# Steps of a gated recurrence, and two sums of weights, each placed behind one split of v's weights

## The chip, the cores and the metric

The kernel runs on one core of a Trainium2 chip. The core has a matrix engine (PE, with PEld loading its weights), a vector engine (DVE), a scalar engine (ACT), a general engine (POOL) and a queue engine (SP); SP and POOL issue the DMAs. Each engine takes its own instructions in order and waits on semaphores for the others. The metric is the time of one execution in microseconds on the device; the median of several executions is compared.

## The reference

One layer of a hybrid block for 512 tokens of width 1024. The normalised input is projected to the inputs of three mixers and their gates; the three results are projected, gated, added, projected again, and a SwiGLU feed-forward layer follows. Two mixers matter here.

```python
xc = causal_conv(u_lru)                          # width 4, per channel
r, i = sigmoid(gate_r(xc)), sigmoid(gate_i(xc))
log_a = -8 * r * softplus(-lam)
a, mult = exp(log_a), sqrt(-expm1(2 * log_a))
h[t] = a[t] * h[t - 1] + mult[t] * i[t] * xc[t]  # the recurrence, along 512 tokens

q, k, v = normalised_x @ w_q, @ w_k, @ w_v       # 1024 x 1024 each, for the attention
```

## The kernel before

Every product in float32 precision is made from three passes of PE over rounded parts: a matrix is split into a high part (ACT rounds it, `whi`, L141) and a low part (DVE subtracts the high part from the raw matrix, `wlo`, L142), and PE adds high*high, high*low and low*high. `split_w` (L134) makes both parts of one piece of weights. The high and the low parts each have three buffers, so that the split of piece n+3 cannot start before PE has used piece n.

The projections to v, k and q (in this order, `VKQ`) go by a Strassen-like scheme with seven products (`ORDER`: 11, 12, S2, S1, S3, S4, 22) in place of eight. Each product has two pieces of weights of 128x1024 (i = 0, 1), and PE makes 12 matmuls of 512 columns for a piece. I write (S4,0) for piece 0 of product S4. `add_seven` (L202) lists the 14 pieces of a unit; the unit numbers un = 0, 1, 2 are v, k and q. Some pieces take more than a split: with product 11 DVE adds two raw blocks to a new block `qs` (L214), which is the raw block of S2; with product S4 DVE adds `qs` to the raw block of 12 (L209), and the sum is the raw block of S4. When the last raw use of a block is over, its buffer takes a block of the next unit (`seven_load`, SP's queue, and an adding DMA on POOL's).

`tok_product` (L820) issues the matmuls. Between products the result is put together from PSUM: `snap` (L841) copies a bank on ACT, `final` (L849) adds or subtracts another bank on DVE. In the traces these are the tile `r` at L843 and L851. Four PSUM tiles exist for this.

The recurrence runs in four chunks of 256 channels (c = 0 to 3), of which the first two are done before v. What remains of chunks 2 and 3 is done while PE works on v:

- `lru_exp`: exponentials and a square root on ACT (L690, L693).
- `lru_decay`: one DVE instruction (L698) and, for chunks 2 and 3, one ACT instruction `1 - t` (L702).
- `lru_input`: two DVE instructions, in these notes "root" (L706) and "product" (L707).
- `lru_scan`: two DVE scans of 512 tokens (L713).
- `lru_store`: a split of the result, ACT (L719) and DVE (L720), and two DMAs to memory on POOL's queue (L722).

The order of each engine's instructions is made by a planner before the run. It follows the program with its own estimate of durations and gives an engine, each time it is free, the ready instruction of the highest priority. Priority is the position in which the program text issues an instruction; `tc.high_priority(n)` moves it n positions up. Splits of v are moved up 320 positions, those of k and q 200, snaps 300, finals and steps of the recurrence not at all. `tc.issue_after(ins)` puts the instructions of its block behind `ins` in the order of that engine, without a wait for its end. Small steps wait in a list `bg`, and `tick` takes one of them at fixed places between the matmuls. `weights` (L297) emits the splits some two pieces ahead of their use.

Before, the list holds for the time of v: decay of chunk 2, decay of chunk 3, the two input steps of chunk 2 (L773), and, from the end of product S3 on, the input steps of chunk 3, scan of chunk 2, scan of chunk 3 behind the fifth last low part emitted until then (L881 to L886), and the two stores (L887).

Of the kernel before, what the change touches and what calls it, by code (L numbers as in the profile page):

```python
# [11 lines left out]
AF = mybir.ActivationFunctionType  # L12
ALU = mybir.AluOpType
# [51 lines left out]
def layer_kernel(ctx: ExitStack, tc: tile.TileContext, x, xt, vecs, w_in, w_qkv7, w_gate7, w_pool, w_rg, w_ig,  # L65
                 w_branch, w_br7, w_out, w_fg, w_fu, w_fd, w_fd7, out):
    nc = tc.nc
    act = nc.scalar.activation
    dve = nc.vector
# [59 lines left out]
        return [wp.tile([P, 1024], F32R, tag=tag, name=n)  # L129
                for tag, n in (("whi", nh), ("wlo", nl))]  # L130

    los = []

    def split_w(raw, shape, n):  # L134
        hi, lo = weight_tiles("whi" + n, "wlo" + n)
        if len(shape) == 3:
            hi, lo = (t.rearrange("p (a b) -> p a b", a=shape[1]) for t in (hi, lo))
        else:
            hi, lo = (t.rearrange("p (a b c) -> p a b c", a=shape[1], b=shape[2]) for t in (hi, lo))
        with tc.high_priority(60):  # L140
            act(hi, raw, AF.Copy)  # L141
            los.append(dve.tensor_tensor(lo, raw, hi.bitcast(F32), ALU.subtract).ins)  # L142
        return hi, lo

# [33 lines left out]
    VKQ = (2, 1, 0)  # L178
# [23 lines left out]
    def add_seven(un, nm, i):  # L202
        u, pieces, shape = UNITS[un]
        last = i == pieces - 1

        def make(n):
            if nm == "S4":
                r = qraw[u, "12", i]
                dve.tensor_tensor(r, r, qraw[u, "S2", i], ALU.add)  # L209
            src = qraw[u, {"S1": "21", "S3": "11", "S4": "12"}.get(nm, nm), i]  # L210
            parts = split_w(src, [P] + list(shape), n)
            if nm == "11":
                qraw[u, "S2", i] = r = b4(list(shape), f"qs{u}{i}")
                dve.tensor_tensor(r, qraw[u, "21", i], src, ALU.add)  # L214
                add = nc.gpsimd.dma_start(src, seven_src(u, "21", i), accum_op=ALU.add)
            if last:
                if un < 3:
                    seven_load(un + 1, {"S1": ("21",), "S3": ("11",), "S4": ("12",), "22": ("22",)}.get(nm, ()))
                elif un == 3 and nm == "11":
                    with tc.issue_after(add.ins):  # L220
                        seven_load(un + 1, ("21", "11"))
                elif un == 3:
                    seven_load(un + 1, {"12": ("12",), "S2": ("22",)}.get(nm, ()))
            return parts
        specs.append((("seven", u, nm, i), make))
# [211 lines left out]
    with ExitStack() as first:  # L437
# [258 lines left out]
        def lru_decay(c):  # L696
            e, t = lru[c]["r"], lru[c]["t"]
            dve.scalar_tensor_tensor(t, e, 1.0, t, ALU.add, ALU.mult)  # L698
            if c < 2:
                dve.tensor_scalar(t, t, -1.0, 1.0, ALU.mult, ALU.add)  # L700
            else:
                act(t, t, AF.Identity, scale=-1.0, bias=1.0)  # L702

        def lru_input(c):
            e, s_ = lru[c]["r"], lru[c]["s"]
            dve.scalar_tensor_tensor(s_, e, 1.0, s_, ALU.add, ALU.mult)  # L706
            dve.tensor_tensor(s_, s_, lru[c]["i"], ALU.mult)  # L707

        def lru_scan(c):
            t, s_ = lru[c]["t"], lru[c]["s"]  # L710
            h = lru[c]["i"]
            for j in range(2):
                dve.tensor_tensor_scan(h[:, j, :], t[:, j, :], s_[:, j, :], 0.0, ALU.mult, ALU.add)  # L713
            lru[c] = h

        def lru_store(c):
            y = lru.pop(c)
            h, l = b4([2, S], f"yh{c}", "b", F32R), y.bitcast(F32R)
            act(h, y, AF.Copy)  # L719
            dve.tensor_tensor(l, y, h.bitcast(F32), ALU.subtract)  # L720
# [49 lines left out]
        gate1(1)  # L770
        step(of(lru_scan, 1)), step(g3, of(lru_store, 0)), step(t3, of(lru_store, 1)), step(of(lru_exp, (2, 3)))
        gate1(2)
        for f, c in ((lru_decay, 2), (lru_decay, 3), (lru_input, 2)):  # L773
            step(of(f, c))
        bg.extend(prepare_t())
        gate1(3)

# [57 lines left out]
        for t in VKQ:  # L835
            ps = {}
            r = {}
# [21 lines left out]
            for nm in ORDER:  # L859
# [38 lines left out]
        for cc in range(2):  # L898
# [6 lines left out]
            lo, hi = slice(0, H), slice(H, S)  # L905
# [7 lines left out]
            for nm in ORDER:  # L913
                ps, half, first_, t, ts_, src, ss = plan[nm]
# [330 lines left out]
    with ExitStack() as third:  # L1245
# [9 lines left out]
        lo, hi = slice(0, H), slice(H, S)  # L1255
# [61 lines left out]
    with ExitStack() as ffn:  # L1317
# [18 lines left out]
        for c in range(4):  # L1336
# [10 lines left out]
            for j in range(2):  # L1347
# [3 lines left out]
                t = x1p[c // 2, j][:, c % 2, :]  # L1351
# [78 lines left out]
        raw = {}  # L1430
# [124 lines left out]
        for m in range(4):  # L1555
            t = fp.tile([P, 2, S], F32, tag="mm", name=f"ps_d{m}")
# [198 lines left out]
```

## Time and profile before

| | us |
|---|---|
| median of three executions | 867.79 (867.76 to 868.42) |
| the profiled execution | 867.76 |
| its span, first to last instruction | 866.0 |
| PE busy | 858.7 (99%) |
| DVE busy | 735.7 (85%) |
| ACT busy | 522.9 (60%) |
| v's matmuls, first to the first of k | 139.19 to 176.73 |

The profile is of one execution; all times in it are microseconds from the first instruction. A busy PE is modelled and is not by itself PE at its best pace, so the starts of successive matmuls are read. A row of the timeline gives the start, the duration, the engine, the line, the operation, the tiles (out<-in), the count, and in brackets the idle time in front of it with what ended it. In a row of the waits stand the total, the count and the longest.

### The profile page before, as it was taken

What the parts mean: (1) busy time and instruction counts of PE and PEld (TensorE: products, weight loads), DVE (VectorE), ACT (ScalarE), POOL (GpSimd) and SP (SyncE); (2) the same over time, 40 slices, a digit from 0 to 9 for tenths busy, and PEclk for the clock granted to TensorE, in tenths of its full rate; (3) what the DMA queues carried; (4) which work ended last, traced back from release to release, by engine and by line L of the source; (5) the groups of instructions that cost most, each with busy time, mean ns of one, the idle gap of its engine ahead of it and who ended that gap; (6) DMA issues with size and microseconds to landing.
All of it is one profiled execution on the core that took longest, in us unless ns stands there. A gap on an engine that the chain in (4) does not pass through costs nothing.

```text
span 866.0 us, 14235 instructions
## 1 busy us (share of the span) xinstructions
PE 858.7 (99%) x5563; PEld 789.7 (91%) x5563; DVE 735.7 (85%) x937; ACT 522.9 (60%) x727; POOL 90.8 (10%) x130
## 2 busy tenths in 40 slices
PE   9999999999999999999999999999999999999998
PEld 7888878888899988889889988889999999999998
DVE  7899897998796698877897787699988888899974
ACT  7554989557966567546665545464555555755642
POOL 1110002232433101000001100000000000121200
PEclk9999999999999999999999999999999999999999
DMA  9586356799592876644727855345633433797913
GB/s 343 164 288 204 98 164 184 228 313 259 172 305 77 245 217 222 216 126 154 218 87 177 195 168 178 100 140 141 166 102 98 121 100 120 225 244 202 196 38 122
DMA packets 116643, 154.08 MB, mean 178 GB/s; under 512 B 8160, under 2 KB 90080, under 8 KB 116576
## 3 DMA queue, kind: packets, MB, share of 16 engines
q1 hardware_dynamic: 103904, 107.30, 38.5%
q0 software_dynamic: 12528, 45.62, 22.2%
q8 instruction: 43, 0.70, 0.3%
q10 hardware_dynamic: 144, 0.26, 0.1%
q14 instruction: 24, 0.20, 0.1%
HBM read 132.71 MB, written 18.87 MB: 175 GB/s over the span
## 4 chain that ended last, share of the span: by engine, by line
PE 88%; DVE 5%; ACT 4%; issue 1%; DMA 1%; SPq 0%; DVEq 0%; ACTq 0%
PE ps_y L315 11%; PE ps_x L315 8%; PE ps_q L830 7%; PE ps_dy L1674 6%; PE ps_dx L1674 5%; PE ps_br L307 3%; PE ps_br L306 3%; PE ps_br L308 3%; PE ps_bY L1299 2%; PE ps_gy L315 2%; PE ps_gate L733 2%; DVE wlo L142 2%; PE ps_bX L1299 2%; PE ps_gx L315 2%; PE ps_pool L307 2%; PE ps_pool L306 2%
## 5 line engine op out<-in xcount | busy, mean ns | idle before, releaser
L141 ACT ACTIVATE whi<-raw 128x1024 fp32r<-128x1024 f32 x69 | 72.8, 1055 | 82.7 <-PE ps_br L307 17.4
L142 DVE TENSOR_TENSOR wlo<-raw,whi 128x1024 fp32r<-128x1024 f32 x69 | 84.2, 1221 | 26.2 <-ACT whi L141 25.5
L142 DVE TENSOR_TENSOR wlo<-qw,whi 128x1024 fp32r<-128x1024 f32 x48 | 58.3, 1220 | 15.8 <-ACT whi L141 15.8
L141 ACT ACTIVATE whi<-qw 128x1024 fp32r<-128x1024 f32 x48 | 50.3, 1053 | 28.2 <-PE ps_q L830 13.2
L1460 ACT ACTIVATE wh_S<-w_S 128x1024 fp32r<-128x1024 f32 x36 | 38.3, 1064 | 30.3 <-PE ps_y L315 18.3
L1580 POOL DMA_DIRECT2D dw<-in_w_down_dram x20 | 16.9, 862 | 305.4 <-DVE wl L1461 243.1
L1461 DVE TENSOR_TENSOR wl_S<-w_S,wh_S 128x1024 fp32r<-128x1024 f32 x36 | 43.8, 1220 | 3.3 <-ACT wh_S L1460 3.3
L1460 ACT ACTIVATE wh<-w 128x1024 fp32r<-128x1024 f32 x27 | 28.6, 1060 | 28.7 <-PE ps_x L315 9.1
L1461 DVE TENSOR_TENSOR wl<-w,wh 128x1024 fp32r<-128x1024 f32 x27 | 32.9, 1220 | 8.2 <-ACT wh L1460 8.2
L1460 ACT ACTIVATE whdS<-dw 128x1024 fp32r<-128x1024 f32 x20 | 21.2, 1061 | 20.6 <-PE ps_dy L1674 10.6
L1113 DVE TENSOR_TENSOR_SCAN E<-K,ahead 128x512 f32<-128x512 f32 (+3 forms) x32 | 25.4, 814 | 5.8 <-ACT K L1109 5.8
L1461 DVE TENSOR_TENSOR wldS<-dw,whdS 128x1024 fp32r<-128x1024 f32 x20 | 24.3, 1222 | 5.1 <-ACT whdS L1460 5.0
L306 PE MATMUL ps_lru<-HH,whi 128*128 128x512 f32 x64 | 24.6, 384 | 0.0
L306 PE MATMUL ps_br<-yph,whi 128*128 128x512 f32 x64 | 24.5, 383 | 0.0
L306 PE MATMUL ps_pool<-HH,whi 128*128 128x512 f32 x64 | 24.5, 383 | 0.0
L306 PE MATMUL ps_br<-yHH,whi 128*128 128x512 f32 x64 | 24.5, 383 | 0.0
L306 PE MATMUL ps_gate<-HH,whi 128*128 128x512 f32 x64 | 24.4, 381 | 0.0
L307 PE MATMUL ps_br<-yHL,whi 128*128 128x512 f32 x64 | 24.4, 381 | 0.0
L307 PE MATMUL ps_lru<-HL,whi 128*128 128x512 f32 x64 | 24.3, 379 | 0.0
L308 PE MATMUL ps_lru<-HH,wlo 128*128 128x512 f32 x64 | 24.3, 379 | 0.0
L307 PE MATMUL ps_gate<-HL,whi 128*128 128x512 f32 x64 | 24.3, 379 | 0.0
L308 PE MATMUL ps_gate<-HH,wlo 128*128 128x512 f32 x64 | 24.3, 379 | 0.0
(740 smaller groups left out, 3435.9 us busy)
## 6 DMA issues: line engine op xcount, KB each, us to landing
raw<-in_w_in_dram SPq DMA_DIRECT2D x31, 512.0 KB, 5.2
qw<-in_w_qkv_dram SPq DMA_DIRECT2D x24, 512.0 KB, 6.8
dw<-in_w_down_dram POOLq DMA_DIRECT2D x20, 512.0 KB, 8.2
w<-in_w_ffn_gate_dram SPq DMA_DIRECT2D x36, 256.0 KB, 3.5
w<-in_w_ffn_up_dram SPq DMA_DIRECT2D x36, 256.0 KB, 4.3
raw<-in_w_branch_dram SPq DMA_DIRECT2D x16, 512.0 KB, 4.0
qw<-in_w_qkv_dram POOLq DMA_DIRECT2D x12, 512.0 KB, 7.5
qd<-r POOLq DMA_DIRECT2D x12, 512.0 KB, 7.1
```

The costliest lines, as they stand in the source:

```text
L141: act(hi, raw, AF.Copy)
L142: los.append(dve.tensor_tensor(lo, raw, hi.bitcast(F32), ALU.subtract).ins)
L306: nc.tensor.matmul(ps, lh, rh, start=start, stop=False, skip_group_check=skip)
L307: nc.tensor.matmul(ps, lh, rl, start=False, stop=False, skip_group_check=skip)
L308: nc.tensor.matmul(ps, ll, rh, start=False, stop=stop, skip_group_check=skip)
L315: nc.tensor.matmul(o, a_[a][:, w, k, :], il2(b_[b][:, k, :]), start=first and n == k == 0, stop=last and n == 2 and k == 3, skip_group_che ...
L830: nc.tensor.matmul(ps[:, a, :], b_[:, k, ts_], il(a_[:, kk, :]), start=first and n == k == 0, stop=n == 2 and k == 3, skip_group_check=True)
L1113: dve.tensor_tensor_scan(E[:, c0:c0 + n][:, ::-1], K[:, c0 + 1:c0 + n + 1][:, ::-1], ahead[:, S - n:][:, ::-1], 0.0, ALU.mult, ALU.add)
L1299: nc.tensor.matmul(o, ah[x_][:, w, k, :], il2(b[k][y_]), start=first_ and n == k == 0, stop=n == 2 and k == 3, skip_group_check=True)
L1460: act(h, src, AF.Copy)
L1461: dve.tensor_tensor(l, src, h.bitcast(F32), ALU.subtract)
L1674: nc.tensor.matmul(o, a_[a][:, w, k0 + k, :], il2(b_[b][:, k, :]), start=first and i == k == 0, stop=last and i == 2 and k == nk - 1, skip ...
```

## The change

`marks` now keeps the high and the low instruction of each split of a unit, and `behind_split` names steps that are issued within the making of one of v's pieces, each behind its low part on DVE. They carry the priority of v's splits.

- behind (12,0): decay of chunk 3
- behind (12,1): root of chunk 2
- behind (S2,0): product of chunk 2
- behind (S2,1): the ACT ends of both decays (`1 - t`), behind the high part on ACT
- behind (S1,1): root of chunk 3
- behind (S4,0): product of chunk 3
- behind (S4,1): scan of chunk 2
- behind (22,0): scan of chunk 3

The two sums for S4 (L209) are put behind the low part of v's (S2,1); for k and q this says nothing. The decay of chunk 2 stays in the list. The two stores enter the list after k's product 11 and not after v's product S3. No arithmetic is changed.

```diff
-    los = []
+    his, los, marks, behind_split = [], [], {}, {}
...
-            act(hi, raw, AF.Copy)
+            his.append(act(hi, raw, AF.Copy).ins)
...
                 r = qraw[u, "12", i]
-                dve.tensor_tensor(r, r, qraw[u, "S2", i], ALU.add)
+                with tc.issue_after(marks[0, "S2", 1][1]):
+                    dve.tensor_tensor(r, r, qraw[u, "S2", i], ALU.add)
...
+            marks[un, nm, i] = his[-1], los[-1]
+            for f in behind_split.pop((un, nm, i), ()):
+                with tc.issue_after(los[-1]):
+                    f()
...
-            else:
+
+        def lru_decay_end(c):
+            t = lru[c]["t"]
+            with tc.issue_after(marks[0, "S2", 1][0]):
                 act(t, t, AF.Identity, scale=-1.0, bias=1.0)
...
-        def lru_input(c):
+        def lru_root(c):
             e, s_ = lru[c]["r"], lru[c]["s"]
             dve.scalar_tensor_tensor(s_, e, 1.0, s_, ALU.add, ALU.mult)
+
+        def lru_product(c):
+            s_ = lru[c]["s"]
             dve.tensor_tensor(s_, s_, lru[c]["i"], ALU.mult)
...
-        for f, c in ((lru_decay, 2), (lru_decay, 3), (lru_input, 2)):
-            step(of(f, c))
+        step(of(lru_decay, 2))
+        behind_split.update({(0, "12", 0): [of(lru_decay, 3)], (0, "12", 1): [of(lru_root, 2)],
+                             (0, "S2", 0): [of(lru_product, 2)],
+                             (0, "S2", 1): [of(lru_decay_end, 2), of(lru_decay_end, 3)], (0, "S1", 1): [of(lru_root, 3)],
+                             (0, "S4", 0): [of(lru_product, 3)], (0, "S4", 1): [of(lru_scan, 2)],
+                             (0, "22", 0): [of(lru_scan, 3)]})
...
-                if (t, nm) == (VKQ[0], "S3"):
-                    def last_scan():
-                        with tc.issue_after(los[-5]):
-                            lru_scan(3)
-
-                    step(of(lru_input, 3)), step(of(lru_scan, 2)), step(last_scan)
+                if (t, nm) == (VKQ[1], "11"):
                     step(of(lru_store, 2)), step(of(lru_store, 3))
```

More of the change, by code (lines that the diff above doesn't have):

```diff
@@ L700, in lru_decay, with lru_input, lru_scan @@
                 dve.tensor_scalar(t, t, -1.0, 1.0, ALU.mult, ALU.add)
-            else:
+        def lru_decay_end(c):
+            t = lru[c]["t"]
+            with tc.issue_after(marks[0, "S2", 1][0]):
                 act(t, t, AF.Identity, scale=-1.0, bias=1.0)
-        def lru_input(c):
+        def lru_root(c):
             e, s_ = lru[c]["r"], lru[c]["s"]
             dve.scalar_tensor_tensor(s_, e, 1.0, s_, ALU.add, ALU.mult)
+        def lru_product(c):
+            s_ = lru[c]["s"]
             dve.tensor_tensor(s_, s_, lru[c]["i"], ALU.mult)
[L709 to L712, printed above, removed]
+        def lru_input(c):
+            lru_root(c)
+            lru_product(c)
+        def lru_scan(c, *js):
+            t, s_, h = (lru[c][n] for n in "tsi")
+            for j in js or range(2):
                 dve.tensor_tensor_scan(h[:, j, :], t[:, j, :], s_[:, j, :], 0.0, ALU.mult, ALU.add)
-            lru[c] = h
         def lru_store(c):
-            y = lru.pop(c)
+            y = lru.pop(c)["i"]
             h, l = b4([2, S], f"yh{c}", "b", F32R), y.bitcast(F32R)
```

## The prediction

> **What bounds the kernel.** I read the page's first part, then what PE waited for, then the starts of v's matmuls, then the chain of work in that stretch, and last DVE's and ACT's rows around the two places.
>
> ```profile
> span 866.0 us, 14235 instructions
> PE 858.7 (99%) x5563; PEld 789.7 (91%) x5563; DVE 735.7 (85%) x937; ACT 522.9 (60%) x727; POOL 90.8 (10%) x130
> ```
>
> PE is the bound: 7.3 us of 866.0 without it. So the change can be worth only what PE loses in the places it touches. The waits of PE by cause (total, times, longest):
>
> ```profile
> PE lg L660 <- DVE xcl L650: 1.4, 1, 1.4
> PE ps_q2S L830 <- DVE wlo L142: 0.5, 1, 0.5
> PE ps_q L830 <- DVE wlo L142: 0.2, 1, 0.2
> ```
>
> In v, k and q (tile ps_q) PE waited twice, both times for a low part from DVE. PE's rows show where, and what each cost:
>
> ```profile
> 139.19 0.38 PE L830 MATMUL ps_q<-whi,HH 128*128 128x512 f32 x1
> ...
> 144.37 0.38 PE L830 MATMUL ps_q<-whi,HH 128*128 128x512 f32 x1
> 144.99 0.48 PE L830 MATMUL ps_q<-wlo,HH 128*128 128x512 f32 x1 [0.24 <-DVE wlo L142]
> 145.31 0.38 PE L830 MATMUL ps_q<-whi,HL 128*128 128x512 f32 x1
> ...
> 165.60 0.38 PE L830 MATMUL ps_q2S<-whi,HH 128*128 128x512 f32 x1
> 166.48 0.48 PE L830 MATMUL ps_q2S<-wlo,HH 128*128 128x512 f32 x1 [0.50 <-DVE wlo L142]
> 166.80 0.38 PE L830 MATMUL ps_q2S<-whi,HL 128*128 128x512 f32 x1
> ...
> 176.73 0.38 PE L830 MATMUL ps_q<-whi,HH 128*128 128x512 f32 x1
> ```
>
> 139.19 to 144.37 is two pieces, 24 matmuls: 0.216 each, 2.59 a piece. At (12,0) the second matmul starts 0.62 after the first, 0.40 late, and the third 0.10 late again: 0.50. At (S4,0) it is 0.66 and 0.10: 0.77 (with rounding). Check: 14 pieces of 2.59 are 36.26, and k starts 37.54 after v: 1.28 lost. That is all there is to win in v, 0.15% of the time.
>
> The chain of work shows why (S4,0) was late:
>
> ```profile
> 159.69 2.25 DVE li L713 x2
> 161.94 1.12 DVE wlo L142
> 163.06 1.27 DVE li L713 x2
> 164.33 0.89 issue
> 165.23 1.21 DVE wlo L142
> 166.44 0.04 issue
> ```
>
> Both scans (2.25 each) ran before the low part of (S4,0). Whether that part could have run sooner, ACT says:
>
> ```profile
> 141.98 1.06 ACT L141 ACTIVATE whi<-qw 128x1024 fp32r<-128x1024 f32 x1
> ...
> 145.40 1.06 ACT L702 ACTIVATE lt<-lt 128x1024 f32<-128x1024 f32 x1
> ...
> 160.62 1.06 ACT L141 ACTIVATE whi<-qw 128x1024 fp32r<-128x1024 f32 x1 [1.53 <-PE ps_q2S L830]
> ...
> 168.72 1.02 ACT L843 ACTIVATE r<-ps_q 128x1024 f32<-128x1024 f32 x1 [1.87 <-DVE r L851]
> ```
>
> The high part of (S4,0) was there at 161.68. DVE needed 3.55 more to begin the low part, and so DVE's order is the cause.
>
> **The change part by part.** DVE's rows give prices and today's order:
>
> ```profile
> 139.17 1.23 DVE L698 SCALAR_TENSOR_TENSOR lt<-lr,lt 128x1024 f32<-128x1024 f32 x1 [1.14 <-ACT ls L693]
> 140.31 2.35 DVE L214 TENSOR_TENSOR qs<-qw,qw 128x1024 f32<-128x1024 f32 x2
> 142.58 1.22 DVE L698 SCALAR_TENSOR_TENSOR lt<-lr,lt 128x1024 f32<-128x1024 f32 x1
> 143.72 1.22 DVE L142 TENSOR_TENSOR wlo<-qw,whi 128x1024 fp32r<-128x1024 f32 x1
> ...
> 150.53 1.22 DVE L142 TENSOR_TENSOR wlo<-qs,whi 128x1024 fp32r<-128x1024 f32 x1
> ...
> 167.48 1.21 DVE L851 TENSOR_TENSOR r<-r,ps_q 128x1024 f32<-128x1024 f32 x1
> 168.61 1.22 DVE L142 TENSOR_TENSOR wlo<-qw,whi 128x1024 fp32r<-128x1024 f32 x1
> 170.73 1.23 DVE L720 TENSOR_TENSOR li<-li,yh 128x1024 fp32r<-128x1024 f32 x1 [0.90 <-ACT yh L719]
> ```
>
> Any 128x1024 instruction takes 1.22, with 1.14 from start to start (142.58 to 143.72). No instruction is added or taken away; only places change. I set DVE's queue against a PE without waits, on which piece n begins at 139.19 + 2.59 n. The low part of a piece has to be ready 0.22 after that. Its high part starts some 0.2 after PE is done with piece n-3 (160.62 against 160.42, the start of piece 8 being 139.19 + 8 x 2.59 + the 0.50), takes 1.06, and the low part 1.22.
>
> *Decay of chunk 3 behind (12,0).* Decay of chunk 2 and the two sums for S2 stay where they are, to 142.58. The low part of (12,0) then goes next, when its high part ends: 141.98 + 1.06 = 143.04. It ends at 144.26; PE wants it at 144.59. The 0.50 goes; margin 0.3. ACT's `1 - t` instructions follow that high part today too, so it does not move.
>
> *Root and product of chunk 2, the sums for S4.* Today six DVE instructions lie between the low parts of (12,0) and (S2,1): root, two sums and splits. After, decay 3, root and product take the place of root and sums: the same count, begun at 143.04 and not 143.72. So (S2,1) begins near 149.9 (150.53 now). Two sums follow, and the low part of (S1,0), at the latest 153.3 to 154.5; PE wants it at 154.95. Margin 0.4, which is gone if a final gets in between: then 0.7 is lost.
>
> *ACT's two ends of the decays.* Two instructions of 1.06 (the second at 145.40 today) move to after the high part of (S2,1), near 148.3 to 150.4. The high part of (S1,0) follows at 150.4 and not 149.8, and its low part waits behind the sums anyway: nothing. The scans need the result at 165 only.
>
> *Root and product of chunk 3.* Root behind (S1,1) runs about 156.7, and the low parts of (S3,0) and (S3,1) end near 159.0 and 160.2, wanted at 160.1 and 162.7. Here DVE catches up with ACT. The high part of (S4,0) starts at 160.1, and nothing stands before its low part: 161.2 to 162.4, wanted at 165.3. The 0.77 goes, margin 2.9. Product 3 fills 162.3 to 163.5.
>
> *The scans.* Their cover is gone from S1 to S3 and is now the end of v: low part of (S4,1) from 163.8, scan 2 from 164.9, low part of (22,0) 167.2 to 168.4 (wanted 170.5), scan 3 to 170.6, low part of (22,1) 170.6 to 171.8 (wanted 173.1, margin 1.3). The final of S3 (167.48 today) has no raised priority and falls behind both scans: 171.7 at the earliest, 4.2 later. ACT's copy at 168.72 waited 1.87 for this final, so it is late next. Its PSUM tile is one of four, and two of the others are free by then (that of the gate before v, and that of 12 after its final), one for 22 and one for k's 11. So I take nothing for it. The bounds are below nothing by 0 (PE has no more to win) and, if k's 11 has to have this tile, the 3.0 of the first rival.
>
> *Stores.* ACT 2 x 1.06, DVE 2 x 1.22 and four DMA issues on POOL leave the end of v for k's 12. On DVE this takes 1.14 + 0.90 from between (22,0) and (22,1), where the scan now goes. POOL's queue has behind them only the adding loads for k's S3 and stores of v, needed some 20 us on or far later. In k, PE did not wait, but DVE had little spare:
>
> ```profile
> 139.19:176.00 36.81, 36.07 (x166) 30.89 (x165) 35.91 (x32) 26.18 (x28) 8.49 (x12) 1.00 0.75 214
> 176.00:212.00 36.00, 36.00 (x169) 31.52 (x168) 31.23 (x34) 23.42 (x29) 10.98 (x11) 1.00 0.93 292
> ```
>
> (Window, its length, busy PE, PEld, DVE, ACT, POOL, clock, DMA share, GB/s.) DVE was busy 35.91 of 36.81 in v and 31.23 of 36.00 in k, so k has 4.8 to take 2 x 1.14 for stores and 1.14 for the final: 3.4. Cost nothing; the upper bound is in the second rival. The DMAs are four of 0.52 MB, 7.2 at the 292 GB/s of that row. They come some 5 us later into a stretch with 0.93 of the DMA engines busy. Of all waits of DVE and ACT between 100 and 300 for these weights, the longest was for the gates, 1.3 at 243, and PE lost nothing by it:
>
> ```profile
> DVE qs L214 <- DMA qw<-in_w_gate_dram: 1.3, 1, 1.3
> ```
>
> [...]
>
> **Sum.** -0.50 - 0.77 = -1.27, the rest nothing. The profiled execution's 867.76 becomes 866.49. It stands 0.03 under the median of the runs, so the median should be 866.5 too, 0.15% less. Differences of under 0.2% (1.7 us) are about what a measurement of this kernel cannot tell from no change, and the forecast lies inside.
>
> **The rivals.**
>
> *The end of v turns late (slower).* Place: the final of S3 and the copy behind it. Besides the scans, the splits and sums for k's pieces carry a raised priority and the final none. In the worst order it comes after the low part of (22,1), k's two first low parts and both sums: 171.7 + 4 x 1.14 = 176.3, its end 177.5, the copy's 178.5. PE wants k's 11 at 175.5. If the planner gave k's 11 that tile, PE stands 3.0: 869.5; and if the low part of (22,1) is overtaken by one more such instruction and a scan half, 1.1 more: 870.6. It decides once the copy ends after 175.5 and the tile is that one. For it: the copy waited for this final already. Against: four tiles, and the final ran at 167.48 with room to spare. 0.19, at 870.0.
>
> *k pays (slower within the bound, or a little over).* DVE executes in order:
>
> ```profile
> 185.49 2.35 DVE L142 TENSOR_TENSOR wlo<-qs,whi 128x1024 fp32r<-128x1024 f32 x2
> ...
> 194.21 0.17 DVE L343 TENSOR_TENSOR krs<-rsqq 128x8 f32<-128x8 f32 x1 [1.56 <-POOL rsqq L342]
> ```
>
> Before the row at 194.21 DVE had no idle of over a microsecond since 139.17. PE would want k's (S2,0) at 176.73 + 4 x 2.59 + 0.22 = 187.3, and it ended at 186.7: 0.6 to spare. Now PE is 1.27 earlier and DVE has 3.4 more to do. If two or three such instructions stand before low parts of k, PE loses up to 2 x 1.14 to 3 x 1.14: 868.8 to 869.9. Against it: k's splits have the raised priority and stores and finals none. [...] By my queue the idle is 1.0 before (S4,0) and 0.3 before (S4,1), both after DVE has caught up. 0.13, of it 0.04 over 869.5.
>
> *The gain comes in part or not at all.* The margins at (12,0) and (S1,0) are 0.3 and 0.4, under one instruction. If the planner lets one 1.14 pass ahead of either, 0.5 to 0.7 stays: 867.0 to 867.2; with both, 867.8. For it: the planner's times are estimates and it had decay 3 ahead of (12,0) before. Against: the edit fixes these very orders. 0.16.
>
> *A wait elsewhere goes too (faster).* PE's 1.4 for `lg` at L660 comes 17 us before v. If the shorter list of steps changed DVE's order there, up to 1.4 more goes: 865.1. Against: the instructions at that place are none of those moved. 0.05.
>
> **How the numbers follow.** Forecast 0.47 (866.0 to 867.0), partial 0.16, k pays 0.13, end of v 0.19, elsewhere 0.05. Faster by over 0.2%: 0.05. Slower: 0.19 + 0.04 = 0.23. Within: 0.47 + 0.16 + 0.09 = 0.72. The range 866.0 to 870.2 leaves out the last case below and half of the end-of-v case above.
>
> **What would show it.** Right: k's first matmul at 175.5 with v's at 139.2; neither wait for `wlo` in PE's list; the low part of (S4,0) within 0.2 of its high part's end; scans after 164; the final of S3 after 171. Wrong: a gap of PE at (22,1), k's 11 or 12 with the copy L843 or `wlo` behind it, or gaps in k that end with `wlo`; any change of DVE's order before 139.

## The result, and the profile after

The changed kernel is slower. The median of six executions is 872.68 us (871.52 to 873.70), and that of the kernel before, on the same chip, 868.20 (867.76 to 868.97): a ratio of 1.0046, with a 95% interval of 1.0035 to 1.0057. The forecast was 866.5, in a range up to 870.2. The profiled execution took 872.78 and its span is 871.0, that is 5.0 more than the span before. All comparisons of single rows below are between two such profiled executions.

The first part of the page of the changed kernel, and what PE waited for in it (total, times, longest):

```profile
span 871.0 us, 14236 instructions
PE 859.3 (99%) x5563; PEld 789.4 (91%) x5563; DVE 735.8 (84%) x937; ACT 523.4 (60%) x727; POOL 88.8 (10%) x130
```

```profile
PE ps_q L847 <- DVE wlo L142: 4.2, 3, 2.9
PE lg L665 <- DVE xcl L655: 1.4, 1, 1.4
...
PE ps_br L312 <- DMA yHL<-ydl: 0.4, 1, 0.4
```

The engines do the same work as before (DVE 735.8, and 735.7 before). The wait at v's (S4,0) (tile `ps_q2S`) and that at v's (12,0) are gone from the list, and three waits for low parts in k and q, 4.2 in total, stand in their place. PE's rows show where they are:

```profile
139.03 0.38 PE L847 MATMUL ps_q<-whi,HH 128*128 128x512 f32 x1
...
175.29 0.38 PE L847 MATMUL ps_q<-whi,HH 128*128 128x512 f32 x1
176.18 0.48 PE L847 MATMUL ps_q<-wlo,HH 128*128 128x512 f32 x1 [0.51 <-DVE wlo L142]
...
196.79 0.38 PE L847 MATMUL ps_q<-whi,hT3h 128*128 128x512 f32 x1
200.04 0.48 PE L847 MATMUL ps_q<-wlo,hT3h 128*128 128x512 f32 x1 [2.88 <-DVE wlo L142]
...
226.21 0.38 PE L847 MATMUL ps_q<-whi,hT2h 128*128 128x512 f32 x1
227.44 0.48 PE L847 MATMUL ps_q<-wlo,hT2h 128*128 128x512 f32 x1 [0.85 <-DVE wlo L142]
```

v now takes 36.26 (139.03 to 175.29), which is the 14 pieces of 2.59 with no wait at all. Successive starts are 0.216 apart without a wait, so PE is 0.67 late at k's (11,0), 3.03 late at k's (S3,0) and 1.01 late at q's (S2,0). From v's first matmul to the first one of the gates behind q PE took 110.06 before (139.19 to 249.25) and 114.33 after (139.03 to 253.36). I use this stretch below to compare kernels. It is 4.27 longer, and that is most of the 5.0. A wait for the load of `yHL` at 356.49, far behind the change, makes 0.60 more.

DVE's rows in v show that the order asked for was made:

```profile
142.93 1.23 DVE L142 TENSOR_TENSOR wlo<-qw,whi 128x1024 fp32r<-128x1024 f32 x1 [0.41 <-ACT whi L141]
144.07 1.22 DVE L703 SCALAR_TENSOR_TENSOR lt<-lr,lt 128x1024 f32<-128x1024 f32 x1
...
161.04 1.23 DVE L142 TENSOR_TENSOR wlo<-qw,whi 128x1024 fp32r<-128x1024 f32 x1 [0.99 <-ACT whi L141]
...
164.77 2.33 DVE L727 TENSOR_TENSOR_SCAN li<-lt,ls 128x512 f32<-128x512 f32 x2
167.02 1.20 DVE L868 TENSOR_TENSOR r<-r,ps_q 128x1024 f32<-128x1024 f32 x1
...
169.27 2.33 DVE L727 TENSOR_TENSOR_SCAN li<-lt,ls 128x512 f32<-128x512 f32 x2
...
172.63 2.36 DVE L215 TENSOR_TENSOR qs<-qw,qw 128x1024 f32<-128x1024 f32 x2
174.90 1.22 DVE L142 TENSOR_TENSOR wlo<-qw,whi 128x1024 fp32r<-128x1024 f32 x1
```

The low part of (12,0) starts at 142.93 with the decay behind it, that of (S4,0) at 161.04, each as soon as its high part is there. The final of S3 (167.02) runs between the scans. Behind the last scan stand one low part and both of k's sums, and so the low part of k's (11,0) starts at 174.90 and PE waits for it.

The large loss is in k. The chain of work that ended last passes there through POOL (start, duration, engine, what; a step on DMA runs from a load's issue to its landing):

```profile
188.85 1.15 DVE wlo L142
190.02 5.44 DMA qw<-in_w_qkv_dram
196.05 0.88 POOL qw L200
196.93 1.70 POOL rsqq L347
198.76 1.23 DVE wlo L142
```

POOL's rows before and after show what stands in another order. First the kernel before, then the changed one:

```profile
191.62 2.56 POOL L342 TENSOR_TENSOR rsqq<-ssq,mhalf 128x8 f32<-128x8 f32 x1 [8.42 <-DVE ssq L798]
194.19 0.92 POOL L200 DMA_DIRECT2D qw<-in_w_qkv_dram  x1
```

```profile
196.05 0.88 POOL L200 DMA_DIRECT2D qw<-in_w_qkv_dram  x1 [6.37 <-DMA qw<-in_w_qkv_dram]
196.63 1.99 POOL L347 TENSOR_TENSOR rsqq<-ssq,mhalf 128x8 f32<-128x8 f32 x1
```

`rsqq` is the first of k's powers (the inverse root of its sums of squares), and the row beside it is q's first adding load, which adds a block onto a block that SP's queue has just loaded. Before, the power came first. After, the adding load comes first, stands 6.37 for the landing of the load that SP issued at 190.02 (its landing takes 5.44, and 3.5 for the same load in the kernel before), and the power behind it in POOL's queue starts at 196.63 and not near 193.7. On DVE the first instruction that uses the power waits 4.98 (1.56 before), and the low part of (S3,0) is behind it:

```profile
185.36 1.22 DVE L733 TENSOR_TENSOR li<-li,yh 128x1024 fp32r<-128x1024 f32 x1
...
187.63 1.22 DVE L733 TENSOR_TENSOR li<-li,yh 128x1024 fp32r<-128x1024 f32 x1
...
192.25 1.22 DVE L814 TENSOR_REDUCE ssq<-sq 128x8 f32<-128x1024 f32 x1
193.50 0.17 DVE L815 TENSOR_SCALAR ssq<-ssq 128x8 f32<-128x8 f32 x1
198.66 0.17 DVE L348 TENSOR_TENSOR krs<-rsqq 128x8 f32<-128x8 f32 x1 [4.98 <-POOL rsqq L347]
198.76 1.23 DVE L142 TENSOR_TENSOR wlo<-qw,whi 128x1024 fp32r<-128x1024 f32 x1
```

Nothing in the diff names the power or the adding load. Their order came from the planner. In the kernel before, the reduction that feeds the power began 2.15 sooner:

```profile
190.10 1.22 DVE L797 TENSOR_REDUCE ssq<-sq 128x8 f32<-128x1024 f32 x1
```

Here it stands behind the two splits of the stores (185.36 and 187.63), and so the power became ready later, while the load ahead of the adding load was issued at the same time (190.02, and 190.14 before). I take it that the planner expected the same and therefore put the adding load first; its estimates were not read.

### The profile page after: what moved, and what is told of

It reads as the page before. It is cut to its first block, busy times and chain, and to the rows that moved or that the text cites. A ratio compares the mean times of both kernels' runs of the same rounds, so it can differ in the third digit from the quotient of the medians.

```text
span 871.0 us, 14236 instructions
## 1 busy us (share of the span) xinstructions
PE 859.3 (99%) x5563; PEld 789.4 (91%) x5563; DVE 735.8 (84%) x937; ACT 523.4 (60%) x727; POOL 88.8 (10%) x130
## 4 chain that ended last, share of the span: by engine, by line
PE 85%; DVE 7%; ACT 3%; DMA 2%; issue 2%; POOL 1%; SPq 0%; DVEq 0%; ACTq 0%; POOLq 0%
PE ps_y L320 11%; PE ps_x L320 8%; PE ps_dy L1686 6%; PE ps_dx L1686 5%; PE ps_q L847 4%; DVE wlo L142 3%; PE ps_br L312 3%; PE ps_br L313 3%; PE ps_br L311 2%; PE ps_bY L1311 2%; PE ps_gy L320 2%; PE ps_gate L746 2%; PE ps_bX L1311 2%; PE ps_gx L320 2%; PE ps_gate L311 2%
```

## The experiments

The table has every run. The stretch is from v's first matmul to the first of the gates, from one profile of each kernel. The waits are PE's own, in v, k and q, by the lateness of the start; those under 0.3 are left out, and so is the 0.10 by which the next matmul is late again. Each ratio is against the kernel before on the same chip. That kernel took 868.03 to 868.69 there, so medians of different rows can differ by some tenths that no edit made; the ratio and the stretch are compared.

| kernel | median | ratio [95%] | stretch | PE late at |
|---|---|---|---|---|
| before | 868.20 | | 110.06 | v (12,0) 0.40, v (S4,0) 0.66 |
| after | 872.68 | 1.0046 [1.0035, 1.0057] | 114.33 | k (11,0) 0.67, k (S3,0) 3.03, q (S2,0) 1.01 |
| power first | 869.22 | 1.0012 [1.0003, 1.0021] | 111.20 | k (11,0) 0.67, k (S3,0) 0.45, q (S2,0) 0.61 |
| before, add first | 871.12 | 1.0030 [1.0021, 1.0040] | 113.20 | v 0.40 and 0.66, k (S3,0) 1.43, q (S2,0) 1.00 |
| stores back | 869.21 | 1.0010 [1.0001, 1.0019] | 110.81 | k (11,0) 0.67, k (S2,0) 0.70 |
| before, only the stores moved | 873.58 | 1.0061 [1.0044, 1.0078] | 115.42 | v 0.39 and 0.66, v (22,1) 1.27, k (S3,0) 2.29, q (S2,0) 1.00 |
| stores after k's S3 | 872.89 | 1.0058 [1.0042, 1.0075] | 114.55 | k (11,0) 0.66, q (S1,0) 1.3 and 1.96 |
| stores after k's S3, sums behind | 873.39 | 1.0055 [1.0041, 1.0069] | 114.08 | q (S1,0) 1.3 and 1.96 |
| after, sums behind | 882.82 | 1.0154 [1.0141, 1.0168] | 122.57 | k (S3,0) 3.41, q (S1,0) 2.99 and 0.93, q (S3,0) 1.04 |
| stores after k's S4, sums behind | 872.70 | 1.0054 [1.0042, 1.0066] | 114.07 | q (S1,0) 2.06 and 1.45 |
| power first, product early | 869.06 | 1.0005 [0.9996, 1.0013] | 111.18 | k (11,0) 0.66, k (S3,0) 0.44, q (S2,0) 0.61 |
| power first, product early, k's sums behind | 869.47 | 1.0006 [0.9994, 1.0018] | 111.19 | k (S3,0) 1.09, q (S2,0) 0.60 |
| power first, product early, k's sums behind, stores at v's end | 868.60 | 1.0000 [0.9990, 1.0009] | 110.72 | k (S2,0) 0.39, q (S2,0) 0.60 |
| stores back, product early | 869.49 | 1.0011 [1.0002, 1.0020] | 110.79 | k (11,0) 0.66, k (S2,0) 0.71 |
| stores after k's S3, q's order held | 874.30 | 1.0074 [1.0060, 1.0089] | 115.81 | k (11,0) 0.66, q (S2,0) 4.46 |
| stores after k's S3, q's order held, k's sums behind | 873.73 | 1.0062 [1.0050, 1.0074] | 115.88 | q (S2,0) 4.45 |

### Is it the pair on POOL's queue?

The first theory (A): the 3.03 at k's (S3,0) comes from the order of that one pair. The rivals (B and C) put it to what the stores bring to k in any case: their time on DVE, and their DMAs beside the load of q. The test has two mirrored halves: the changed kernel with the power held first, and the kernel before with the adding load held first.

```diff
 (changed kernel)
...
                 if nm == "21":
-                    nc.gpsimd.dma_start(r, seven_src(u, "22", i), accum_op=ALU.add)
+                    with tc.issue_after(pows[-1]) if n == 2 else ExitStack():
+                        nc.gpsimd.dma_start(r, seven_src(u, "22", i), accum_op=ALU.add)
...
-        nc.gpsimd.tensor_tensor(t, ms, e, ALU.pow)
+        pows.append(nc.gpsimd.tensor_tensor(t, ms, e, ALU.pow).ins)
```

> The changed kernel with one pair on POOL's queue exchanged back: k's first power (for the scales of k) goes ahead of the first adding load of q's block 21, as in the kernel before. Theory A (the power waits on POOL behind an adding load that waits for a DMA, DVE waits for the power, and the low part of k's (S3,0) stands behind that on DVE): DVE's wait of 4.98 for the power falls to about 2.5 (0.1 + the power's 2.5), PE's gap of 3.0 at k's (S3,0) to about 1.2, and the gap of 1.0 in q gets smaller: 2 to 3 us less than the changed kernel, about 870. Theory B (the two stores' work on DVE in k is what costs, 2 x 1.22 and their place): POOL's order does not matter, 872.5 as the changed kernel, gap of 3.0 unchanged. Theory C (the stores' DMAs take bandwidth from q's load): as B, since the DMAs are the same.

What differs from the changed kernel is the pair's order on POOL, the place of the low part of (S3,0) beside DVE's use of the power, and on ACT the places of the scalings that follow from the power. PE's order is the same. POOL's and DVE's rows of this kernel:

```profile
193.76 1.67 POOL L350 TENSOR_TENSOR rsqq<-ssq,mhalf 128x8 f32<-128x8 f32 x1 [4.07 <-DVE ssq L818]
195.63 0.92 POOL L203 DMA_DIRECT2D qw<-in_w_qkv_dram  x1 [0.20 <-issue]
```

```profile
195.46 0.17 DVE L351 TENSOR_TENSOR krs<-rsqq 128x8 f32<-128x8 f32 x1 [1.78 <-POOL rsqq L350]
```

DVE's wait falls from 4.98 to 1.78, the stretch from 114.33 to 111.20, and the ratio from 1.0046 to 1.0012. That is more than theory A had expected (about 870), and B and C, by which the order does not matter, have fallen in that form. The adding load starts at 195.63 and not at 196.05: it loses nothing by coming second.

```diff
 (kernel before)
-                    nc.gpsimd.dma_start(r, seven_src(u, "22", i), accum_op=ALU.add)
+                    add = nc.gpsimd.dma_start(r, seven_src(u, "22", i), accum_op=ALU.add)
+                    if n == 2:
+                        q_adds.append(add.ins)
...
-            parts = split_w(src, [P] + list(shape), n)
+            with tc.issue_after(square[-1]) if (un, nm, i) == (1, "S3", 0) else ExitStack():
+                parts = split_w(src, [P] + list(shape), n)
...
-        eng.tensor_tensor(y, t, t, ALU.mult)
+        square.append(eng.tensor_tensor(y, t, t, ALU.mult).ins)
...
+            if not q_adds:
+                bg.append(lambda: post2(t, i, j, r, s_))
+                return
...
+            with tc.issue_after(q_adds[0]):
+                rsqrt(...)
```

> The mirror: the kernel before, with the same pair on POOL exchanged the other way (the adding load of q ahead of k's first power) and, as in the changed kernel, the low part of k's (S3,0) between the first and the second small instruction of the scales. Theory A: the power starts only when q's load has landed, some 4.8 us after its issue at 190.1, so near 195; DVE waits 4 to 5 and not 1.6, the low part of (S3,0) ends near 199 where PE wants it at 198.1: a gap of about 1 at that place, 869.0 to 870. Theories B and C: no gap, 868.0 to 868.4.

```profile
195.55 0.93 POOL L202 DMA_DIRECT2D qw<-in_w_qkv_dram  x1 [11.86 <-DMA qw<-in_w_qkv_dram]
196.17 2.00 POOL L347 TENSOR_TENSOR rsqq<-ssq,mhalf 128x8 f32<-128x8 f32 x1
```

With no step of the recurrence moved, the swap makes the stretch 3.14 longer (113.20 against 110.06), and the other half took away 3.13. The median of 871.12 is above the 869.0 to 870 that theory A had given: 1.43 at k's (S3,0) was near the expected 1, and the 1.00 at q's (S2,0) was not in it. That the two halves agree so closely is in part chance, since they are made up in another way: the first took 2.58 away at (S3,0) and 0.40 at q's (S2,0).

The transfers have a share in the size. The load that the adding load waits for lands 4.3 after its issue here and 5.4 in the changed kernel. In the six kernels whose stores enter the list after k's 11 it takes 5.0 to 5.5, and in the nine others, the kernel before among them, 3.4 to 3.5. So the moved stores' DMAs, issued from 184.67 to 189.15, go with a landing that is 1.5 to 2.1 later. With the power first nothing waits for that (the landing takes 5.0 there, and the stretch is 111.20); with the adding load first, the power and DVE do. By my estimate from these rows, a landing after 3.5 would have brought the power 1.9 sooner and left some 1.1 of the 3.03.

### Which part of the change makes the swap, and does the rest gain?

```diff
 (changed kernel)
-                if (t, nm) == (VKQ[1], "11"):
+                if (t, nm) == (VKQ[0], "S3"):
                     step(of(lru_store, 2)), step(of(lru_store, 3))
```

> The changed kernel with only the two stores put back to the end of v's product S3 in the list; splits, scans and sums stay in their new places. The planner then has the power ahead of the adding load again. Theory A: no gap at k's (S3,0); both gaps of v stay away (1.27 less than the kernel before), the 0.77 at k's (11,0) stays, because both sums for S2 still go ahead of its low part: 867.4 to 867.9. Theory B: also no gap there; the two differ in the other runs. If the moved scans and not the stores were the cause, the gap of 3.0 stays: over 870.

```diff
 (kernel before)
                     step(of(lru_input, 3)), step(of(lru_scan, 2)), step(last_scan)
+                if (t, nm) == (VKQ[1], "11"):
                     step(of(lru_store, 2)), step(of(lru_store, 3))
```

> The kernel before with only the two stores moved to the end of k's product 11. The planner then has the adding load ahead of the power, as in the changed kernel. Theory A: gaps of v stay (0.5 and 0.77), and a gap of 2 to 3 comes at k's (S3,0): 870.5 to 872. If the scans' new places are what delays k: 868.0 to 868.5.

The move of the stores makes the swap by itself: with the stores back the power is first again by the planner's own order and (S3,0) has no wait, and with only the stores moved the pair is swapped and DVE waits 5.01 for the power:

```profile
199.70 0.17 DVE L343 TENSOR_TENSOR krs<-rsqq 128x8 f32<-128x8 f32 x1 [5.01 <-POOL rsqq L342]
```

Moved alone, the stores cost 5.36 of the stretch, more than the whole change (4.27) and more than I had expected (873.58, and 870.5 to 872). One piece of that was not in the changed kernel: k's two sums ran ahead of the low part of v's (22,1), the second waited 2.25 there for its load, and PE stood 1.27.

But the rest of the change gains nothing even with the stores in their old place in the list. I expected 867.4 to 867.9 and found 869.2. Both waits of v are gone there too, and 0.67 at k's (11,0), which the forecast had counted in, and 0.70 at k's (S2,0), which it had not, have come. The stores' splits still ran in k (176.76 and 179.03, with k begun at 176.00). In the changed kernel with the power first it is 0.67, 0.45 and 0.61. This is the second finding: k and q take back what v gives.

### Can the stores go somewhere else?

If the stores' place ahead of the reduction is the trouble, they can enter the list later. Four kernels did this or put sums behind low parts:

```diff
 (stores after k's S3)
-                if (t, nm) == (VKQ[1], "11"):
+                if (t, nm) == (VKQ[1], "S3"):
                     step(of(lru_store, 2)), step(of(lru_store, 3))

 (sums behind, for v, k, q and the gates)
-                dve.tensor_tensor(r, qraw[u, "21", i], src, ALU.add)
+                with tc.issue_after(los[-1]):
+                    dve.tensor_tensor(r, qraw[u, "21", i], src, ALU.add)

 (stores after k's S4, with the sums behind)
-                if (t, nm) == (VKQ[1], "11"):
+                if (t, nm) == (VKQ[1], "S4"):
```

> The changed kernel with the two stores put into the list one step later, after k's product S3 and not after k's product 11. The planner then puts both stores behind the first reduction of k and the first power ahead of q's adding load. Theory A with the stores' share of it (the stores delay the reduction, and so the planner lets the adding load pass the power): no gap at k's (S3,0), none of 1.0 in q, gaps of v gone, 0.77 at k's first piece left: about 0.5 less than the kernel before, 867.3 to 867.8 beside 868.0. If the scans at the end of v are a cause of their own: a gap in k stays, over 868.5.

> As the kernel with the late stores, and each sum for S2 (of v, k, q and the gates) put behind the low part of its own piece of 11, so that k's first low part no longer waits for both sums (2.27 on DVE). Expected: the 0.77 at k's (11,0) goes too: 866.6 to 867.2, some 1.2 under the kernel before. If the sums are needed earlier than that for a later product, a new gap in k's S2 or S3 gives it back.

> The changed kernel with only the sums for S2 behind the low parts of their own pieces; stores and the order of power and adding load as in the changed kernel. Expected: the gap of 0.67 at k's first piece goes, the gap of about 3 at k's (S3,0) stays or grows by what PE is earlier (0.8), because DVE's wait for the power ends with the landing of q's load, at an absolute time: 872 to 873, no gain. If the two gaps were independent: 0.8 less than the changed kernel, 871.8.

> As the kernel with late stores and moved sums, with the stores one product later still, after k's product S4. If what the stores need is a stretch in which DVE has room, S4 and the start of q are as good as S3: within 0.3 of the other, 866.6 to 867.4. If they collide with q's reductions and powers: a gap in q, 868 or more.

None of them helps. The three with late stores took 872.7 to 873.4, where I had forecast 866.6 to 867.8, and the one with the sums behind and the stores where the change has them took 882.8 against 872 to 873. In that last one the pair on POOL is swapped as in the changed kernel, the wait at (S3,0) is 3.41, the planner changed PE's order in q too, and two drops of PE's granted clock, to 0.50 and 0.54, come on top, of which the last section tells. With the stores later the waits at (S3,0) are gone, and with the sums behind also that at (11,0), so that k runs without a wait. Then PE waits in q: 3.3 or 3.5 in all, and with the sums behind a drop of the granted clock to 0.50 adds to it (about 1.7 with the stores after k's S3). The planner had also changed PE's own order in q and put five matmuls of S1 ahead of S2 (nine in the kernel that took 882.8). PE's rows of the kernel with the stores after k's S3 and the sums behind:

```profile
224.26 0.38 PE L848 MATMUL ps_q<-whi,HL 128*128 128x512 f32 x1
225.78 0.48 PE L848 MATMUL ps_q0S<-whi,hT1h 128*128 128x512 f32 x1 [1.15 <-ACT whi L141]
228.06 0.62 PE L848 MATMUL ps_q0S<-wlo,hT1h 128*128 128x512 f32 x1 [1.80 <-DVE wlo L142]
228.48 0.63 PE L848 MATMUL ps_q0S<-whi,hT1l 128*128 128x512 f32 x1
```

Two theories were left, PE's changed order (E) or DVE's time (F). To tell them apart I held q's S1 behind S2:

```diff
 (stores after k's S3)
+                        with tc.issue_after(state["s2"]) if (t, nm) == (VKQ[2], "S1") else ExitStack():
                             mm = nc.tensor.matmul(...)
+                        if nm == "S2":
+                            state["s2"] = mm.ins
```

> The changed kernel with the stores entering the list after k's S3, and q's matmuls of S1 held behind those of S2, so that PE's order of matmuls is that of the kernel before. With the stores there and no such hold PE had the first S1 matmuls of q ahead of S2, stood 1.3 and 1.96 for S1's parts, and the median was 872.9. If that was PE's order (theory E), both gaps go, and what is left is the 0.66 at k's (11,0): about 868.5. If the stores' splits make q's low parts late in any order (theory F), a gap of 1 to 2 comes at q's (S2,0) or (S1,0) in its place: 870 to 872.

> The same, and each of k's two sums for S2 behind the low part of its own piece of product 11, for k alone. Theory E: no wait of PE for v's or k's weights is left, 868.0 or up to 1 less, the first of these kernels that could beat the one before. Theory F: as without the sums, since what PE saves in k it waits for in q: 870 to 872.

PE's order of all matmuls is then that of the kernel before, and it is no better: 874.3 and 873.7, above both theories' forecasts. PE's, ACT's and DVE's rows of the first of the two:

```profile
222.99 0.38 PE L848 MATMUL ps_q<-whi,HL 128*128 128x512 f32 x1
227.67 0.48 PE L848 MATMUL ps_q<-whi,hT2h 128*128 128x512 f32 x1 [4.30 <-ACT r L863]
```

```profile
225.64 1.06 ACT L813 ACTIVATE sq<-r 128x1024 f32<-128x1024 f32 x1 [1.18 <-DVE r L871]
226.61 1.01 ACT L863 ACTIVATE r<-ps_q 128x1024 f32<-128x1024 f32 x1
```

```profile
224.39 1.22 DVE L871 TENSOR_TENSOR r<-r,ps_q 128x1024 f32<-128x1024 f32 x1
```

q's S2 goes on in the bank of 11, and so it needs ACT's copy of that bank first. The copy (226.61) stands behind a square of one of k's results, and the square waits for DVE's final of k at 224.39. DVE had been at work since 205.94 with no pause of over 0.2, the two splits of the stores among it. So theory E has fallen: PE's changed order was not the cause. F is supported only in part. The wait is again behind DVE, but at a final, a square and a copy and not at a low part, and it is larger than F had it (4.46, not 1 to 2). The final came 84.84 after v's first matmul, and 75.20 in the kernel before. That is 9.6 later, while the two splits of the stores take 2.3 of DVE, so the planner's place for the final counts as well. How much of the wait is the stores' own was not separated.

### Can DVE be given time at the end of v?

In the changed kernel and in the one with the power first DVE stood about 1.0 for the high part of v's (S4,0). The next two kernels put the product of chunk 3 into this gap, one of them with k's sums behind; a third, with both, moved the stores to the end of v, and a fourth took the product alone with the stores back:

```diff
 (power first)
-(0, "S1", 1): [of(lru_root, 3)],
-                             (0, "S4", 0): [of(lru_product, 3)], (0, "S4", 1): [of(lru_scan, 2)],
+(0, "S1", 1): [of(lru_root, 3)], (0, "S3", 1): [of(lru_product, 3)],
+                             (0, "S4", 1): [of(lru_scan, 2)],

 (k's sums behind)
+                with tc.issue_after(los[-1]) if un == 1 else ExitStack():
                     dve.tensor_tensor(r, qraw[u, "21", i], src, ALU.add)

 (stores at v's end)
-                if (t, nm) == (VKQ[1], "11"):
+                if (t, nm) == (VKQ[0], "22"):
```

> The kernel with the power first, and product of chunk 3 put behind the low part of v's (S3,1) and no longer behind that of (S4,0). In the kernel with the power first DVE stood 1.02 for the high part of (S4,0) at 161.04, and the product ran behind it. If the gaps left at the start of k come from DVE being late out of v (theory D: v's end is too full), the product fills this idle, DVE comes out of v about 1.0 earlier, the 0.67 at k's (11,0) and the 0.45 at k's (S3,0) go, and the median is 869.2 - 1.1 = 868.1 or a little less. If those gaps come from the order within k (the two sums ahead of the low part of (11,0), the stores' splits ahead of the reduction), whatever the hour, they stay and the median is 869.2.

> The kernel before this one in the list, and with it each of k's two sums for S2 behind the low part of its own piece of product 11 (for k alone, so PE's own order in q is that of the kernel before the change). Theory D: nothing more is won, 868.1 as without it. If the order of sums and low parts is the cause, only here the 0.67 at k's (11,0) goes, and this kernel is 0.7 under the one without it.

> The kernel before this one in the list, with the two stores entering the list after v's product 22 and not after k's product 11; the power stays first on POOL. Their two splits then run two or three places earlier on DVE. Theory D: DVE has the same work, and the low part of k's (S3,0) is no later; 868.1 or up to 0.4 less, with no gap of PE over 0.5 in k. If the stores' place before or behind the finals of k counts, a gap at k's (S2,0) of about 0.7 comes, as with the stores at the end of v's S3.

> The kernel with the stores put back to the end of v's S3 (no pin of the power, it is first by the planner's own order), and product of chunk 3 behind the low part of v's (S3,1). There the gaps were 0.67 at k's (11,0) and 0.70 at k's (S2,0). Theory D: DVE comes out of v 1.0 earlier, both go, 869.2 - 1.4 = 867.8, at or a little under the kernel before. If the gaps belong to the order and not to the hour, 869.2.

The product came into the gap, and DVE did not come out of v earlier. DVE's rows of the first of the four:

```profile
161.36 1.22 DVE L142 TENSOR_TENSOR wlo<-qw,whi 128x1024 fp32r<-128x1024 f32 x1
163.91 1.22 DVE L142 TENSOR_TENSOR wlo<-qw,whi 128x1024 fp32r<-128x1024 f32 x1 [1.34 <-ACT whi L141]
```

The idle time moved one piece on, in front of the low part of (S4,1), whose high part ends at the same time as before. From there on the order is unchanged, and all waits in k and q with it: a stretch of 111.18, nothing won against 111.20. The reason I had given for a gain (theory D) has fallen: what sets DVE's end of v is the high part of (S4,1) and the time of the nine instructions between its low part and that of k's (11,0), not the work ahead of it. The fourth kernel says the same: its two gaps stayed (0.66 and 0.71, 869.49).

With k's sums behind, the 0.67 at k's (11,0) goes, as the order of sums and low parts would have it, and the wait at (S3,0) grows from 0.44 to 1.09. The stretch is 111.19 with and 111.18 without. PE's gain at one piece is its wait at the next, since DVE works from 163.85 to 193.9 with no pause of over 0.2. The best version has the stores at the end of v. Its wait at (S3,0) is gone and one of 0.39 at k's (S2,0) has come, as the rival to theory D had it (0.7). Its stretch is 110.72, and its time that of the kernel before, 1.0000 (0.9990 to 1.0009). No kernel tried is faster than the one before.

## Why the prediction was wrong

**v's two waits, -0.50 and -0.77: right.** Both are gone, and v takes 36.26, the 14 pieces of 2.59. k began 36.26 after v's first matmul and not 37.54, which is the 1.28 of the forecast.

**The steps in v: right in order, wrong in one detail.** The low part of (S4,0) started at 161.04 (said: 161.2). The scans start at 164.77 and 169.27 (said: 164.9, and one that ends at 170.6). The final of S3 did not fall behind both scans (171.7) but between them (167.02), and so the first rival (the end of v turns late, by the copy and the PSUM tile) did not occur. But the final's 1.1 then stood ahead of the low part of (22,1), which started at 171.52 (said: 170.6). Both of k's sums follow it, and the low part of k's (11,0) ended at 176.12, where PE wanted it at 175.5: this is the 0.67. The forecast gave no time for that part. The kernels with k's sums behind it have no wait there.

**"Stores. [...] POOL's queue has behind them only the adding loads for k's S3 and stores of v, needed some 20 us on or far later": this step failed.** POOL's queue also has k's powers, whose first is needed by DVE at once. The step counted the stores' own four issues on POOL and the work behind them, and stopped there. It did not ask what two splits of 1.14 on DVE do to the hour of the reduction, what waits for the reduction on POOL, and which of POOL's other instructions the planner would now put ahead of it. The row for it was in the prediction (DVE's 1.56 for `rsqq` at 194.21), and was read as DVE's idle time and not as a place where DVE waits for POOL with a low part behind it. The measured price of the swap is 3.13 to 3.14 us of the stretch, from both sides.

**"Cost nothing" for the stores in k, against 4.8 to spare: wrong as well.** The sum over a stretch (31.23 busy of 36.00) was taken for room at each place. In k the free time lies behind 193, after a run of about 30 us with none (in the changed kernel from 163.6 to 193.7). With the pair put right, the stretch is 111.20, and three units of 36.26 would be 108.8. So 2.4 of waits are in k and q, where there were none before, against the 1.3 taken away in v. The second rival (k pays, 868.8 to 869.9) had this part right, in size (the kernel with the power first took 869.2) and in the main in mechanism: instructions ahead of k's low parts on a full DVE. It put them down to the stores and the final; with the stores back at their old place in the list the stretch is still 110.81, so their later place makes only 0.4 of the 2.4. It was given 0.13.

**The transfers: without a place in the sum.** The load of q that the adding load waits for was issued at 190.02 and at 190.14 before, so its issue was not delayed. Its landing took 5.4 and not 3.5, 1.9 more; the longest wait for a load of weights that the prediction had read was 1.3, and its sum has no term for one. In the order of the kernel before this costs nothing; behind the swap it is part of DVE's wait. The wait for `yHL` at 356.49, 0.60, is no step of the prediction. It varies from under 0.15 to 1.47 among the kernels without a pattern that these runs show, and its cause stays open.

So the mechanism of the gain was right, and most of the loss came by an order of two instructions that the change does not name. The forecast had no case for an order on POOL that changes, and the range ended at 870.2. One smaller reading was off without a result for the sum: five DVE instructions, and not six, lay between the low parts of (12,0) and (S2,1) before; the time from one to the other (six starts of 1.14) was used rightly.

## What to carry to other kernels

When a step is moved past a place where a planner decides, list what feeds on the moved engine time on each in-order queue, compute instructions on a queue that also issues DMAs included: an instruction that waits for a landing holds whatever is behind it (6.37 here), and two instructions that trade places there can cost more than the work that was moved (3.13 here, against 2.3 of DVE for the two splits). Free time summed over a stretch is no cover; ask for the longest run of the engine without a pause (about 30 us here), and which low part stands at its end. Where one engine is busy at every such place, a wait that is removed can come back at the next one (with k's sums behind, 0.66 less at k's (11,0) and 0.65 more at (S3,0)). I would expect only less work on that engine to keep the gain; no run here tried it.

## What the runs showed of the hardware that I had not expected

*The clock after short gaps.* PE's granted clock stayed at 1.00 after the idle time of 2.88 at k's (S3,0) in the changed kernel: the matmuls behind it start 0.21 to 0.22 apart. In the kernel with the sums behind it fell after one of 3.25, and in the kernel with the stores after k's S3 and the sums behind it fell after two of 1.15 and 1.80 with one matmul between, as it did after 1.90 and 1.29 with the stores after k's S4 (0.50 from 226 to 228). By window (length, PE, PEld, DVE, ACT, POOL, granted clock, DMA share, GB/s), first the changed kernel, then the one with the sums behind, then the other:

```profile
200.00:201.00 1.00, 0.95 (x4) 0.86 (x5) 0.93 (x4) 0.43 (x2) 0.00 (x0) 1.00 1.13 209
```

```profile
200.80:202.20 1.40, 0.00 (x0) 0.00 (x0) 1.37 (x3) 0.00 (x0) 0.89 (x1) 0.59 0.90 173
202.20:206.20 4.00, 3.98 (x9) 3.19 (x10) 1.52 (x4) 3.46 (x8) 0.00 (x0) 0.50 1.03 228
...
208.00:210.00 2.00, 2.00 (x11) 1.76 (x10) 1.23 (x1) 0.43 (x1) 0.10 (x1) 1.00 0.59 135
```

```profile
228.00:230.00 2.00, 1.94 (x5) 1.56 (x6) 2.00 (x8) 1.48 (x3) 0.33 (x1) 0.57 0.41 100
```

The starts are then 0.43 apart and not 0.216. In the last kernel this lasts from 228.06 to 231.5 and costs about 1.7 more on top of the gaps; with the sums behind it lasts from about 201 to 208, and a second time from 235.0 to 238.5 behind gaps of 2.83 and 0.78. The kernels with q's order held have such a drop too, behind their 4.30 (0.52 and 0.50 from 228 to 231), so their stretches hold about 1.7 or more of slow matmuls. In these runs a single gap of 2.88 came without a drop, single gaps of 3.25 and 4.30 with one, and two gaps of under 2 us each (1.15 and 1.80, 1.90 and 1.29) with one as well. What decides between these cases was not shown.

*A power on POOL.* The first power of k, of 128x8, took 1.66 to 2.62 us in these kernels, more than a 128x1024 instruction of DVE (about 1.22), and DVE stood at least 1.56 for it in every one of them. It sits on DVE's path in k with or without the change; the change only made it wait its turn.
